# Two layers of a mixer and a feed-forward network in float32 on one core: low-rank products and key norm by tokens, and other banks and factor times where stages join

## The chip, the core and the metric

The kernel runs on one core of a Trainium2 chip. TensorE (PE) multiplies matrices into PSUM, VectorE (DVE), ScalarE (ACT) and GpSimd (POOL) work element by element, SyncE (SP) issues most transfers. Times are device microseconds of one execution. Each version runs several times; the median counts. One execution is also recorded by the hardware profiler: the profile and the trace are of that one.

## The reference, cut to what matters

256 tokens of width 1024 go through two layers. A layer adds to h a mixer of four branches (RWKV-7, dilated attention, mLSTM, HGRN-2, each gated and projected), then a gated feed-forward network of width 2816. All is float32.

```
for l in range(2):
    xn = rmsnorm(h, norm_mix_g[l]); z = xn @ w_in[l]
    merged = sum over 4 branches of sigmoid(gate_b + b_gate) * (y_b @ p_b)
    h = h + merged @ w_out[l]
    xn = rmsnorm(h, norm_ffn_g[l])
    u, gt = split(causal_dwconv(xn @ w_up[l])); h = h + (silu(gt) * u) @ w_down[l]
out = rmsnorm(h, final_norm_g)

# RWKV branch: what the change touches
logw = -softplus(-(w0 + tanh(wl) @ w2)) - 0.5      # wl, al: 32 wide; gl: 64 wide
a = sigmoid(a0 + al @ a2);  g = sigmoid(gl) @ g2
kk = k * k_k;  kk = kk * rsqrt(sum over a head's 64 columns of kk*kk + 1e-12)
```

## The kernel before, in words

**Weights.** All weights stream from HBM in 312 groups, most of 128 x 1024 float32 (raw, three buffers). For each product ACT rounds a group to the PE's one-pass type (hi, L301), DVE subtracts to get the rest (lo, L302), and each product is three matmuls: hi with the left high half, lo with it, hi with the left low half (mm3, L351 to L353). hi and lo have four buffers each. A request for group i issues transfers up to i + 6 and splits up to i + 4.

**Order.** The program text is in one sequence; a scheduler sets the order on each engine when the kernel is built, by priorities, so an edit in one stage can move rows on all engines. Work of the branches runs as background generators (rwkv, hgrn, attn, mlstm) that a step in the weight products advances. An engine runs its rows in that fixed order: a row whose inputs are late holds up all rows behind it on that engine.

**Norms by factor.** A norm is not applied to h ahead of a product. First products of a layer take u = (xh, xl), h times the norm's gain, and the result is multiplied by the row factor R when it is taken from PSUM. The factor: ACT squares h, sums into acc (L418); row_factor multiplies acc by ones on PE (psrm or psrf, L424), DVE scales (rcm, L426), POOL raises to -1/2 (L427); row_bcast spreads rcm over partitions with two float32 matmuls with an identity (psbm, L434) and ACT copies (Rm, L437). Later products take s = (sh, sl), blocks of h times gain and R (scaled_block, split_scaled, L440 to L454).

**Start of a layer (rw_cols, L605).** The RWKV columns are four groups of products, rw0 to rw3 (weight groups 0 to 6 in layer 0, 157 to 163 in layer 1), in three PSUM banks of the pool pmm that all stages share; zr takes them with R (L610). Between those evacuations stand the eight scaled blocks xsc. In layer 0 row_factor follows rw1 and R is made after the first half of rw2; in layer 1 row_factor follows rw0 and R stands within rw1. Then come the HGRN columns (hgq, hgf, and hgt by tokens), and after them gate products (gate). A second PSUM pool (PS["rw"], PS["mx"]) holds small tiles.

**RWKV's low-rank part (L669 to L734).** lort (the three low-rank matrices) and the activations are split by casts into lw and la, stacked so that hi and lo products sum in one matmul of 96 rows; psw and psa are two matmuls each, psg four. The key norm multiplies squares rsq (256 columns a token) by a block-diagonal matrix of ones on PE (pss), then ACT takes Ln and Exp with -0.5 (nk, L733 and L734, two table loads). Vt holds the values by tokens, copied by ACT from transposes (pv, L773, L781).

**Feed-forward.** 22 pairs of groups up0 to up21; the first five take u, R comes after up1's first half; POOL multiplies xsc by Rf and subtracts halves; then conv, silu, product af and its split ahi, alo (L1453 to L1459). In layer 1 the last product is by tokens, two row halves h by two column halves q (pso), and finish and emit add h, sum squares (ss), take the power and scale (L1492 to L1509).

Of the kernel before, what the change touches and what calls it, by code (L numbers as in the profile page):

```python
# [221 lines left out]
def trunk(tc, x, wst, prm, rows, lora, fing, cfd, cid, out, dbg=None, depth=DEPTH):  # L222
# [160 lines left out]
    def tok_group(name, cols, mid=None):  # L383

        pss = [pmm.tile([128, 512], F32, name=f"{name}{h}", tag="mm") for h in range(2)]
        for kh in range(4):
            hi, lo = w_next()
            for h in range(2):
                for k in range(2):
                    kk = kh * 2 + k  # L390
                    mm3(pss[h][:, :cols], X["s"][0][:, kk, h * 128:(h + 1) * 128], X["s"][1][:, kk, h * 128:(h + 1) * 128],
# [100 lines left out]
    for l in range(depth):  # L492
        with ExitStack() as lx:
# [12 lines left out]
            with ExitStack() as mxs:  # L506
# [48 lines left out]
                def project(b, kn, m2, quiet=False):  # L555
# [18 lines left out]
                    if m2 == 0:  # L574
                        mop = mp("mop", bufs=1)
                        pad(mop, "padm", 128)
                        X["m"] = (mop.tile([128, KB, T], F32R, name="mh"), mop.tile([128, KB, T], F32R, name="ml_"))
# [25 lines left out]
                R = None  # L603

                def rw_cols():  # L605
                    nonlocal R
# [5 lines left out]
                    def scale(ms):  # L612
                        for m in ms:
                            if m % 2 == 0:
                                tmp = gtp.tile([128, 2, T], F32, name="xsc", tag="gt")
                            scaled_block(m, P("gmix", m) if l else pr0[:, m:m + 1], R, tmp[:, m % 2, :])

                    u = X["u"]
                    ps0 = ct_group("rw0", outer=(l > 0), a=u)
                    rc = None  # L620
# [29 lines left out]
                def rwkv():  # L650
# [18 lines left out]
                    lw = rw.tile([128, 4, 256], F32R, name="lw", tag="bk")  # L669
                    hi_ = lambda d, s_: ac.copy(d, s_)  # L670
                    lo_ = lambda d, s_, h_: ve.tensor_tensor(d, s_, h_.bitcast(F32), op=OP.subtract)
                    for i, r in ((0, 0), (1, 32)):
                        src = lort[r:r + 32, :]
# [881 lines left out]
```

## Time and profile before

| what | value |
|---|---|
| median of 3 runs | 955.33 us (949.43 to 957.17) |
| the profiled execution | 955.37 us |
| its span | 953.5 us |
| granted PE clock in it | 0.993 of full speed |
| PE, DVE, ACT, POOL busy | 97%, 76%, 60%, 24% |
| instructions | 22170 |

The profile shows by engine how much of the span it was busy, who waited for whom, the chain of waits that ends last, and in a timeline each row with its start and length in us. In square brackets stands how long the engine stood idle ahead of a row and what it waited for last. A row may stand for several instructions (x4). A matmul's length contains its way through the array; starts of consecutive rows are closer together.

### The profile page before, as it was taken

The page shows a single profiled execution, that of the slowest core. Times are in us where ns is not written, and L with a number is a line of the kernel's source. Part 1 is how long each engine was busy: PE and PEld are TensorE (multiplying, and loading weights), DVE is VectorE, ACT ScalarE, POOL GpSimd, SP SyncE. Part 2 cuts the span into 40 slices and gives each one's busy share as a digit, 9 for nine tenths or more (in the row PEclk, how much of TensorE's full clock was granted, in tenths as well). Part 3 has the DMA queues.
Part 4 walks back from the last instruction along what each step waited for, and adds up shares of the span by engine and source line. Part 5 has one row for each costly group of instructions (what it writes and reads, how often), then busy time and mean ns, then how long its engine had stood idle before and what let it go on. Part 6 is the DMA issues. An engine that isn't in the chain of part 4 may idle for free.

```text
span 953.5 us, 22170 instructions
## 1 busy us (share of the span) xinstructions
PE 928.6 (97%) x9072; PEld 880.2 (92%) x9072; DVE 720.6 (76%) x1136; ACT 569.7 (60%) x968; POOL 226.3 (24%) x226
## 2 busy tenths in 40 slices
PE   8899999999999999999999999999999999999996
PEld 6888999999999999999998899999989999999885
DVE  6898566678688998876678975567768889988643
ACT  7784455665466676664478644555745667866533
POOL 2500141111317621110142004211103474211002
PEclk9999999999999999999999999999999999999998
DMA  7544444345475476556555434444536646656561
GB/s 276 177 135 132 126 149 142 134 154 166 144 216 183 146 221 199 187 174 197 189 172 181 147 98 125 154 155 122 188 123 189 201 138 215 230 189 200 182 193 66
DMA packets 48981, 160.12 MB, mean 168 GB/s; under 512 B 5872, under 2 KB 7408, under 8 KB 48752
## 3 DMA queue, kind: packets, MB, share of 16 engines
q1 hardware_dynamic: 46800, 155.03, 50.9%
q10 hardware_dynamic: 1728, 2.62, 0.9%
q8 instruction: 71, 1.16, 0.5%
q0 software_dynamic: 352, 1.06, 0.4%
q14 instruction: 30, 0.25, 0.1%
HBM read 156.06 MB, written 1.05 MB: 165 GB/s over the span
## 4 chain that ended last, share of the span: by engine, by line
PE 74%; DVE 10%; ACT 5%; POOL 4%; issue 4%; DMA 2%; POOLq 0%; SPq 0%; ACTq 0%; DVEq 0%
PE up L353 6%; PE up L351 6%; PE up L352 6%; PE gate L351 6%; PE gate L353 5%; PE gate L352 5%; PE dn L351 4%; PE dn L353 4%; PE dn L352 4%; DVE lo L302 4%; POOL sl L446 2%; POOL xsc L1432 2%; ACT hi L301 2%; DMA raw<-in_wst_dram 1%; PE at L351 1%
## 5 line engine op out<-in xcount | busy, mean ns | idle before, releaser
L302 DVE TENSOR_TENSOR lo<-raw,hi 128x1024 fp32r<-128x1024 f32 (+4 forms) x316 | 377.8, 1201 | 164.7 <-ACT hi L301 155.7
L301 ACT CAST hi<-raw 128x1024 fp32r<-128x1024 f32 (+4 forms) x316 | 307.4, 978 | 275.2 <-PE up L352 47.8
L353 PE MATMUL up<-sh,lo 128*128 128x256 f32 x544 | 152.2, 280 | 0.8 <-DVE lo L302 0.8
L351 PE MATMUL up<-sh,hi 128*128 128x256 f32 x544 | 152.0, 279 | 0.0
L352 PE MATMUL up<-sl,hi 128*128 128x256 f32 x544 | 151.9, 279 | 0.0
L351 PE MATMUL gate<-sh,hi 128*128 128x256 f32 x512 | 146.5, 286 | 0.0
L353 PE MATMUL gate<-sh,lo 128*128 128x256 f32 x512 | 143.0, 279 | 0.0
L352 PE MATMUL gate<-sl,hi 128*128 128x256 f32 x512 | 142.6, 279 | 0.0
L353 PEld LDWEIGHTS up<-sh,lo 128*128 128x128 f32 x544 | 103.4, 190 | 1.4 <-DVE lo L302 1.4
L352 PEld LDWEIGHTS up<-sl,hi 128*128 128x128 f32 x544 | 102.2, 188 | 0.0
L351 PEld LDWEIGHTS up<-sh,hi 128*128 128x128 f32 x544 | 102.2, 188 | 0.0
L351 PEld LDWEIGHTS gate<-sh,hi 128*128 128x128 f32 x512 | 96.5, 188 | 2.3 <-issue 0.2
L353 PEld LDWEIGHTS gate<-sh,lo 128*128 128x128 f32 x512 | 96.2, 188 | 0.6
L352 PEld LDWEIGHTS gate<-sl,hi 128*128 128x128 f32 x512 | 96.3, 188 | 0.4
L1457 POOL TENSOR_TENSOR af<-sf,cvf 128x256 f32<-128x256 f32 x44 | 45.9, 1043 | 157.8 <-ACT sf L1455 157.8
L1453 DVE SCALAR_TENSOR_TENSOR cvf<-up,pr,cvf 128x255 f32<-128x255 f32 (+1 forms) x136 | 65.1, 479 | 2.4
L572 POOL TENSOR_TENSOR merged<-merged,gt 128x512 f32<-128x512 f32 x16 | 26.6, 1666 | 114.3 <-DVE gt L570 114.3
L352 PE MATMUL dn<-alo,hi 128*128 128x256 f32 x176 | 49.5, 281 | 0.0
L353 PE MATMUL dn<-ahi,lo 128*128 128x256 f32 x176 | 49.5, 281 | 0.0
L351 PE MATMUL dn<-ahi,hi 128*128 128x256 f32 x176 | 49.4, 281 | 0.0
L352 PE MATMUL up<-xl,hi 128*128 128x256 f32 x160 | 44.8, 281 | 0.0
L353 PE MATMUL up<-xh,lo 128*128 128x256 f32 x160 | 44.6, 280 | 0.1
(468 smaller groups left out, 2370.0 us busy)
## 6 DMA issues: line engine op xcount, KB each, us to landing
raw<-in_wst_dram SPq DMA_DIRECT2D x254, 512.0 KB, 3.5
raw<-in_wst_dram SPq DMA_DIRECT2D x16, 448.0 KB, 3.2
raw<-in_wst_dram SPq DMA_DIRECT2D x26, 256.0 KB, 2.8
raw<-in_wst_dram SPq DMA_DIRECT2D x8, 392.0 KB, 3.2
zrot<-zrot ACTq DMA_DIRECT2D x24, 64.0 KB, 3.1
cft<-in_cf_dram SPq DMA_DIRECT2D x1, 1041.0 KB, 7.4
hT<-in_x_dram SPq DMA_DIRECT2D x4, 256.0 KB, 6.0
raw<-in_wst_dram SPq DMA_DIRECT2D x8, 128.0 KB, 2.6
```

Of the source, the lines that this page charges most:

```text
L301: ac.copy(hi[:, c], r[:, c])
L302: ve.tensor_tensor(lo[:, c], r[:, c], hi[:, c].bitcast(F32), op=OP.subtract)
L351: te.matmul(o, lh, rh, start=first, stop=False)
L352: te.matmul(o, lh, rl, start=False, stop=False)
L353: te.matmul(o, ll, rh, start=False, stop=last)
L446: gp.tensor_tensor(lo[:, m, :], tmp, h[:, m, :].bitcast(F32), op=OP.subtract)
L572: gp.tensor_tensor(mo, mo, g, op=OP.add)
L1432: gp.tensor_tensor(xsc[:, m, :], xsc[:, m, :], R, op=OP.mult)
L1453: ve.scalar_tensor_tensor(cv[:, n, d:], z[:, n, 0:T - d], P("fcw", 44 * i + cj), cv[:, n, d:], op0=OP.mult, op1=OP.add)
L1457: gp.tensor_tensor(a_, s, cv[:, 0, :], op=OP.mult)
```

## The change

In the RWKV branch psw, psa and psg become plain float32 matmuls of lort and the activations; lw, la and their casts and subtractions go. The key norm is taken by tokens: four float32 matmuls of 128 squares with two columns of ones (psn), DVE adds 1e-12, POOL raises to -1/2 (rn), and eight float32 matmuls with an identity spread it over partitions (pnk), from where DVE multiplies; Ln, Exp and their table loads go. In rw_cols rw2 and rw3 use banks of PS["rw"] in place of pmm; R follows the whole of rw1 in layer 1 and the middle of rw2 holds row_factor in layer 0. The scaled blocks move behind the evacuations into hg_cols. hgf and hgt take u in both layers, and the row factor is applied at evacuation (rc, and rch for the Tanh). In the feed-forward, up0 uses pmm, row_factor moves into the middle of up1 and R behind it. At the end the last 512 columns are two blocks of 256 (po2), each summed and added into ss as it ends; the other product with gr for the second token half moves from POOL to DVE. padm is 32 bytes.

The diff:

```diff
--- before.py
+++ after.py
@@ -363,7 +363,7 @@
...
-        pl = PS["mx"] if pool_tag == "mx" else pmm
+        pl = PS[pool_tag] if pool_tag else pmm
@@ -600,24 +601,23 @@
...
+                def scale(ms):
@@ -630,20 +630,19 @@
...
-                        ps1 = ct_group("rw1", a=u, mid=get_R)
+                        ps1 = ct_group("rw1", a=u)
+                        get_R()
...
-                        get_rc()
-                        ps2 = ct_group("rw2", a=u, mid=get_R)
+                        ps2 = ct_group("rw2", a=u, mid=get_rc, pool_tag="rw")
+                        get_R()
...
-                    scale(range(0, 4))
...
-                    scale(range(4, 8))
-                    evac(2, ps2 or ct_group("rw2", a=u))
+                    evac(2, ps2 or ct_group("rw2", a=u, pool_tag="rw"))
...
-                    ps = pmm.tile([128, 2, T], F32, name="rw3", tag="mm")
+                    ps = PS["rw"].tile([128, 2, T], F32, name="rw3", tag="rw")
@@ -666,38 +665,17 @@
...
-                        hi_(lw[0:32, i], src)
-                        hi_(lw[32:64, i], src)
-                        lo_(lw[64:96, i], src, lw[r:r + 32, i])
-                    hi_(lw[64:128, 2], lort[64:128, :])
-                    hi_(lw[0:64, 2], lort[64:128, :])
-                    lo_(lw[64:128, 3], lort[64:128, :], lw[64:128, 2])
...
-                        te.matmul(psw[:, n, :], lw[0:96, 0, n * 128:(n + 1) * 128], la[0:96, 0], start=True, stop=True)
-                        te.matmul(psa[:, n, :], lw[0:96, 1, n * 128:(n + 1) * 128], la[0:96, 1], start=True, stop=True)
+                        te.matmul(psw[:, n, :], lort[0:32, n * 128:(n + 1) * 128], lr[0:32, :], start=True, stop=True)
+                        te.matmul(psa[:, n, :], lort[32:64, n * 128:(n + 1) * 128], zm[32:64, 6, :], start=True, stop=True)
@@ -714,24 +692,26 @@
...
-                        te.matmul(psg[:, h, :], la[:, 2, h * 128:(h + 1) * 128], lw[:, 2], start=True, stop=False)
-                        te.matmul(psg[:, h, :], la[64:128, 2, h * 128:(h + 1) * 128], lw[64:128, 3], start=False, stop=True)
+                        te.matmul(psg[:, h, :], lr[64:128, h * 128:(h + 1) * 128], lort[64:128, :], start=True, stop=True)
...
-                    pss = PS["rw"].tile([128, 2, T], F32, name="pss", tag="rw")
-                    te.matmul(flat(pss), C("bd"), flat(sq), start=True, stop=True)
+                    psn = PS["rw"].tile([128, 2, 2, 2], F32, name="psn", tag="rw")
+                    for h in range(2):
+                        for n in range(2):
+                            te.matmul(psn[:, h, n, :], sq[:, n, h * 128:(h + 1) * 128], C("ind"), start=True, stop=True)
...
+                    ve.tensor_scalar(rn[:, 0, :], psn.rearrange("p h n q -> p (h n q)"), 1e-12, None, op0=OP.add)
+                    gp.tensor_tensor(rn[:, 1, :], rn[:, 0, :], nhalf, op=OP.pow)
...
-                    ac.activation(nk, pss, AF.Ln, bias=eps12)
-                    ac.activation(nk, nk, AF.Exp, scale=-0.5)
@@ -750,8 +730,16 @@
...
+                    pnk = PS["rw"].tile([128, 2, T], F32, name="pnk", tag="rw")
+                    for n in range(2):
+                        for h in range(2):
+                            for q in range(2):
+                                i = h * 4 + n * 2 + q
+                                te.matmul(pnk[q * 64:q * 64 + 64, n, h * 128:(h + 1) * 128], rn[:, 1, i:i + 1].to_broadcast([128, 64]),
+                                          ident, start=True, stop=True)
...
-                    ve.tensor_tensor(kk, kkr, nk, op=OP.mult)
+                    ve.tensor_tensor(kk, kkr, pnk, op=OP.mult)
@@ -952,20 +940,19 @@
...
-                        ps = ct_group("hg" + nm, **({"a": X["u"]} if direct else {}))[0][1]
+                        ps = ct_group("hg" + nm, a=X["u"])[0][1]
...
-                            ve.tensor_tensor(z, ps, bc2(R, 2), op=OP.mult)
...
+                        ve.tensor_tensor(z, ps, bc2(R, 2), op=OP.mult)
...
-                    pss = tok_group("hgt", 512)
+                        scale(range(i * 4, i * 4 + 4))
+                    pss = tok_group("hgt", 512, a=X["u"])
+                    rch = zp.tile([128, 2], F32, name="rch")
+                    ve.tensor_scalar(rch, rc[:, 0:2], 0.5, None, op0=OP.mult)
...
-                        ac.activation(V[:, h, :], pss[h][:, 0:256], AF.Copy)
-                        ac.activation(tg[:, h, :], pss[h][:, 256:512], AF.Tanh, scale=0.5)
+                        ac.activation(V[:, h, :], pss[h][:, 0:256], AF.Copy, scale=rc[:, h:h + 1])
+                        ac.activation(tg[:, h, :], pss[h][:, 256:512], AF.Tanh, scale=rch[:, h:h + 1])
@@ -1414,14 +1401,10 @@
...
-                        ps0 = ct_group("up0", outer=True, quiet=True, pool_tag="mx", a=u)
-                        rc = row_factor(f"f{l}")
-                        def get_R():
...
-                            R = row_bcast(f"f{l}", rc)
-                        ps1 = ct_group("up1", quiet=True, pool_tag="mx", a=u, mid=get_R)
+                        ps0 = ct_group("up0", outer=True, quiet=True, a=u)
+                        rcf = []
+                        ps1 = ct_group("up1", quiet=True, pool_tag="mx", a=u, mid=lambda: rcf.append(row_factor(f"f{l}")))
+                        R = row_bcast(f"f{l}", rcf[0])
@@ -1477,35 +1460,42 @@
...
-                    pso = [[PS["mx"].tile([128, 512], F32, name=f"dn{h}{q}", tag="mx") for q in range(2)] for h in range(2)]
+                    pso = [[PS["mx"].tile([128, 512], F32, name=f"dn{h}{q}", tag="mx") for q in range(2 - h)] for h in range(2)]
+                    po2 = {part: pmm.tile([128, 256], F32, name=f"dn11{part}", tag="mm") for part in (0, 256)}
...
+                                mm3(po2[part], ahi[:, k, t], alo[:, k, t], hi[:, c], lo[:, c], k == 0, k == NJ - 1)
...
-                        ve.tensor_tensor(o_, pso[h][q], htt[:, h, c], op=OP.add)
...
+                        ve.tensor_tensor(o_[:, b], po2[b0] if h and q else pso[h][q], htt[:, h, c], op=OP.add)
...
-                        ac.activation(sq, o_, AF.Square, accum_out=ss[:, q:q + 1])
+                        ac.activation(sq[:, b], o_[:, b], AF.Square, accum_out=ss[:, i:i + 1])
+                        ve.tensor_scalar(ss[:, 4 + i:5 + i], ss[:, i:i + 1], 1.0 / D, ss[:, 3 + i:4 + i] if i else 1e-6, op0=OP.mult, op1=OP.add)
...
-                            gp.tensor_tensor(o_, o_, gr[:, c], op=OP.mult)
...
-                        ve.tensor_tensor(ss[:, 2:3], ss[:, 0:1], ss[:, 1:2], op=OP.add)
-                        ve.tensor_scalar(ss[:, 2:3], ss[:, 2:3], 1.0 / D, 1e-6, op0=OP.mult, op1=OP.add)
...
+                            (ve if h else gp).tensor_tensor(o_[:, b], o_[:, b], gr[:, c], op=OP.mult)
...
+                        gp.tensor_tensor(r, ss[:, 4 + i:5 + i], nhalf[:, 0:1], op=OP.pow)
```

On PE, at the start of layer 0, before: psrm (L424) stands 27 rows above psbm; the rows here are those around psbm, with hi4 and lo4 as weight group 4 (rw2).

```order
L353 MATMUL rw2_351<-xh_112,lo4_233 128x256
L351 MATMUL rw2_351<-xh_112,hi5_265 128x256
L352 MATMUL rw2_351<-xl_113,hi5_265 128x256
L434 MATMUL psbm0_383<-ident_t_70,rcm0_348 128x128 x2
L353 MATMUL rw2_351<-xh_112,lo5_266 128x256
```

Now, in the same place: psrm follows the last row of rw1 and psbm follows it by two rows of rw2. The 24 rows of rw2 that stood between psrm and psbm follow psbm.

```order
L353 MATMUL rw1_260<-xh_112,lo3_202 128x256
L425 MATMUL psrm0_377<-ones_77,acc_84 128x1 x2
L351 MATMUL rw2_345<-xh_112,hi4_232 128x256
L352 MATMUL rw2_345<-xl_113,hi4_232 128x256
L435 MATMUL psbm0_413<-ident_t_70,rcm0_380 128x128 x2
L353 MATMUL rw2_345<-xh_112,lo4_233 128x256
```

DVE at the start of layer 0, before (rcm is the row factor by tokens, zr the RWKV columns, xsc the scaled blocks, lo4 to lo8 the low halves of weight groups):

```order
L302 TENSOR_TENSOR lo4_233<-raw4_193,hi4_232 128x1024
L426 TENSOR_SCALAR rcm0_348<-psrm0_345 128x2
L302 TENSOR_TENSOR lo5_266<-raw5_195,hi5_265 128x1024
L302 TENSOR_TENSOR lo6_318<-raw6_230,hi6_317 128x1024
L302 TENSOR_TENSOR lo7_356<-raw7_263,hi7_355 128x1024
L302 TENSOR_TENSOR lo8_391<-raw8_315,hi8_390 128x1024
L610 TENSOR_TENSOR zr_185<-rw0_187,Rm0_386 128x2x256
L454 SCALAR_TENSOR_TENSOR xsc_419<-hT_73,pr0_71,Rm0_386 128x256
L454 SCALAR_TENSOR_TENSOR xsc_430<-hT_73,pr0_71,Rm0_386 128x256
L610 TENSOR_TENSOR zr_185<-rw1_260,Rm0_386 128x2x256
L454 SCALAR_TENSOR_TENSOR xsc_439<-hT_73,pr0_71,Rm0_386 128x256
L454 SCALAR_TENSOR_TENSOR xsc_447<-hT_73,pr0_71,Rm0_386 128x256
```

And now: both zr and the four scaled blocks stand ahead of lo6, and rch behind lo4. Before, lo4 to lo8 stood ahead of all of them.

```order
L427 TENSOR_SCALAR rcm0_380<-psrm0_377 128x2
L302 TENSOR_TENSOR lo4_233<-raw4_193,hi4_232 128x1024
L950 TENSOR_SCALAR rch_819<-rcm0_380 128x2
L302 TENSOR_TENSOR lo5_266<-raw5_195,hi5_265 128x1024
L617 TENSOR_TENSOR zr_185<-rw0_187,Rm0_416 128x2x256
L617 TENSOR_TENSOR zr_185<-rw1_260,Rm0_416 128x2x256
L455 SCALAR_TENSOR_TENSOR xsc_567<-hT_73,pr0_71,Rm0_416 128x256
L455 SCALAR_TENSOR_TENSOR xsc_578<-hT_73,pr0_71,Rm0_416 128x256
L455 SCALAR_TENSOR_TENSOR xsc_680<-hT_73,pr0_71,Rm0_416 128x256
L455 SCALAR_TENSOR_TENSOR xsc_688<-hT_73,pr0_71,Rm0_416 128x256
L302 TENSOR_TENSOR lo6_318<-raw6_230,hi6_317 128x1024
L302 TENSOR_TENSOR lo7_350<-raw7_263,hi7_349 128x1024
```

ACT at the start of layer 1, before (hi161 to hi164 are weights, Rm1 the row factor spread over partitions, xsc the scaled blocks):

```order
L670 CAST lw_6849<-lort_6498 64x256 x2
L301 CAST hi161_6533<-raw161_6440 128x1024
L301 CAST hi162_6594<-raw162_6525 128x1024
L301 CAST hi163_6629<-raw163_6531 128x1024
L437 COPY Rm1_6625<-psbm1_6622 128x256
L451 ACTIVATE xsc_6670<-hT_73,pr_6483 128x256
```

And now: Rm1 stands behind hi164, one cast later than before. In the feed-forward of both layers Rf likewise moved behind one more cast.

```order
L301 CAST hi162_6587<-raw162_6518 128x1024
L301 CAST hi163_6617<-raw163_6524 128x1024
L301 CAST hi164_6656<-raw164_6585 128x1024
L438 COPY Rm1_6648<-psbm1_6645 128x256
L452 ACTIVATE xsc_6871<-hT_73,pr_6476 128x256
L452 ACTIVATE xsc_6973<-hT_73,pr_6476 128x256
```

## Rows read from the trace of the kernel before

**Rows 1.** The chain that ended last, by engine, from the page.

```profile
PE 74%; DVE 10%; ACT 5%; POOL 4%; issue 4%; DMA 2%; POOLq 0%; SPq 0%; ACTq 0%; DVEq 0%
```

**Rows 2.** Waits of PE: line, releaser: us in total, times, longest.

```profile
PE rw L351 <- DVE zr L610: 4.0, 2, 2.7
...
PE pv L773 <- ACT Vt L781: 1.8, 2, 1.1
...
PE psrf L424 <- DVE acc L418: 1.4, 2, 1.2
...
PE up L353 <- DVE lo L302: 0.8, 3, 0.4
```

**Rows 3.** Timeline of PE, start of layer 0: start, length, what [idle before].

```profile
22.21 0.61 PE L424 MATMUL psrm<-ones,acc 128*128 128x1 f32 x4 [0.58 <-DVE acc L418]
...
23.49 0.39 PE L353 MATMUL rw<-xh,lo 128*128 128x256 f32 x1 [0.33 <-DVE lo L302]
...
26.34 0.61 PE L434 MATMUL psbm<-ident_t,rcm 128*128 128x128 f32 x4
26.70 0.37 PE L353 MATMUL rw<-xh,lo 128*128 128x256 f32 x1
...
32.20 0.40 PE L351 MATMUL rw<-xh,hi 128*128 128x256 f32 x1 [2.65 <-DVE zr L610]
```

**Rows 4.** Stretches: length, busy time of each engine, granted clock, DMA share, GB/s.

```profile
33.00:36.50 3.50, 3.50 (x19) 3.50 (x19) 3.50 (x6) 3.17 (x9) 3.50 (x5) 0.53 0.40 140
```

**Rows 5.** Timeline of ACT, start of layer 0.

```profile
29.24 1.04 ACT L301 CAST hi<-raw 128x1024 fp32r<-128x1024 f32 x1 [0.76 <-DMA raw<-in_wst_dram]
30.19 0.37 ACT L437 COPY Rm<-psbm 128x256 f32<-128x256 f32 x1
```

**Rows 6.** Timeline of DVE, start of layer 0.

```profile
31.46 0.69 DVE L610 TENSOR_TENSOR zr<-rw,Rm 128x512 f32<-128x512 f32 x1
32.06 1.93 DVE L454 SCALAR_TENSOR_TENSOR xsc<-hT,pr,Rm 128x256 f32<-128x256 f32 x2
```

**Rows 7.** Timeline of PE around psw and around psg and pss.

```profile
47.17 0.36 PE L699 MATMUL psw<-la,lw 96*128 96x256 f32 x1 [0.48 <-DVE la L671]
...
53.61 0.39 PE L351 MATMUL hgt<-hi,sh 128*128 128x512 f32 x1
53.84 0.28 PE L717 MATMUL psg<-lw,la 128*128 128x256 f32 x1
...
54.98 1.13 PE L726 MATMUL pss<-rsq,cft 128*128 128x512 f32 x2
...
56.18 0.40 PE L353 MATMUL hgt<-hi,sl 128*128 128x512 f32 x1
```

**Rows 8.** Timeline of PE: two small float32 products elsewhere.

```profile
89.59 0.95 PE L807 MATMUL psq<-cft,prod 128*128 128x2 f32 x8
...
228.40 1.57 PE L1309 MATMUL pS<-cv 64*128 64x256 f32 x12
```

**Rows 9.** Groups of ACT by line: count, busy us, mean ns.

```profile
L670 ACT CAST lw<-lort 32x256 fp32r<-32x256 f32 (+1 forms) x12 | 4.8, 403 | 1.8 <-DMA lort<-in_lora_dram 1.6
...
L733 ACT ACT_TABLE_LOAD x2 | 2.6, 1283 | 0.0
```

**Rows 10.** Timeline of POOL: the power of the row factor.

```profile
23.59 1.62 POOL L427 TENSOR_TENSOR rcm<-rcm,nhalf 128x2 f32<-128x2 f32 x1 [2.42 <-DVE rcm L426]
```

**Rows 11.** Stretches behind the starts of layers 0 and 1, columns as above.

```profile
50.00:75.00 25.00, 24.86 (x219) 21.23 (x217) 22.89 (x44) 19.94 (x34) 0.00 (x0) 1.00 0.52 159
525.00:550.00 25.00, 23.93 (x257) 21.71 (x256) 23.14 (x46) 16.63 (x31) 0.86 (x2) 1.00 0.43 136
```

**Rows 12.** Timeline after the last matmul, of DVE and POOL.

```profile
945.52 0.69 DVE L1492 TENSOR_TENSOR o__12474<-dn,htt 128x512 f32<-128x512 f32 x1 [0.64 <-PE dn L353]
...
947.06 0.64 DVE L1500 TENSOR_TENSOR ss<-ss 128x1 f32<-128x1 f32 x1 [0.85 <-ACT osq L1494]
...
947.97 0.55 POOL L1502 TENSOR_TENSOR ss<-ss,nhalf 128x1 f32<-128x1 f32 x1 [0.29 <-DVE ss L1501]
```

More of the change, by code (lines that the diff above doesn't have):

```diff
@@ L381, in ct_group, with tok_group @@
         return [(slice(0, 2), ps)]
-    def tok_group(name, cols, mid=None):
+    def tok_group(name, cols, mid=None, a=None):
+        ah, al = a or X["s"]
         pss = [pmm.tile([128, 512], F32, name=f"{name}{h}", tag="mm") for h in range(2)]
@@ L390, in tok_group @@
                     kk = kh * 2 + k
-                    mm3(pss[h][:, :cols], X["s"][0][:, kk, h * 128:(h + 1) * 128], X["s"][1][:, kk, h * 128:(h + 1) * 128],
+                    mm3(pss[h][:, :cols], ah[:, kk, h * 128:(h + 1) * 128], al[:, kk, h * 128:(h + 1) * 128],
                         hi[:, k * cols:(k + 1) * cols], lo[:, k * cols:(k + 1) * cols], kk == 0, kk == 7)
@@ L575, in project @@
                         mop = mp("mop", bufs=1)
-                        pad(mop, "padm", 128)
+                        pad(mop, "padm", 32)
                         X["m"] = (mop.tile([128, KB, T], F32R, name="mh"), mop.tile([128, KB, T], F32R, name="ml_"))
@@ L601, in trunk @@
                 gp.memset(zr[:, :, 0:1], 0.0)
-                R = None
+                R = rc = None
+                def scale(ms):
+                    for m in ms:
+                        if m % 2 == 0:
+                            tmp = gtp.tile([128, 2, T], F32, name="xsc", tag="gt")
+                        scaled_block(m, P("gmix", m) if l else pr0[:, m:m + 1], R, tmp[:, m % 2, :])
                 def rw_cols():
-                    nonlocal R
+                    nonlocal R, rc
                     def evac(g, ps):
@@ L1486, in down, with finish @@
                         t = slice(h * 128, h * 128 + 128)
+                        if h and q:
+                            for part in parts:
+                                c = slice(512 + part, 768 + part)
+                                mm3(po2[part], ahi[:, k, t], alo[:, k, t], hi[:, c], lo[:, c], k == 0, k == NJ - 1)
+                            return
                         mm3(pso[h][q], ahi[:, k, t], alo[:, k, t], hi[:, c], lo[:, c], k == 0, k == NJ - 1)
-                    def finish(h, q, ss):
-                        c = slice(q * 512, q * 512 + 512)
-                        o_ = op_.tile([128, 512], F32, name="o_", tag=f"o{h}{q}")
-                        ve.tensor_tensor(o_, pso[h][q], htt[:, h, c], op=OP.add)
+                    def finish(h, q, ss, o_, b0=0, b1=512, i=0):
+                        b, c = slice(b0, b1), slice(q * 512 + b0, q * 512 + b1)
+                        ve.tensor_tensor(o_[:, b], po2[b0] if h and q else pso[h][q], htt[:, h, c], op=OP.add)
@@ L1504, in emit @@
+                        return i
+                    def emit(h, o2, ss, i):
+                        r = ss[:, 8:9]
+                        gp.tensor_tensor(r, ss[:, 4 + i:5 + i], nhalf[:, 0:1], op=OP.pow)
+                        ac.activation(o2[0], o2[0], AF.Copy, scale=r)
                         nc.scalar.dma_start(out[0, h * 128:(h + 1) * 128, 0:512], o2[0])
                         if h == 0:
-                            ac.activation(o2[1], o2[1], AF.Copy, scale=ss[:, 3:4])
+                            ac.activation(o2[1], o2[1], AF.Copy, scale=r)
@@ L1517, in trunk @@
                     for h in range(2):
-                        ss = op_.tile([128, 4], F32, name="ss", tag=f"ss{h}")
-                        o2 = []
+                        ss = op_.tile([128, 10], F32, name="ss", tag=f"ss{h}")
+                        o2 = [op_.tile([128, 512], F32, name="o_", tag=f"o{h}{q}") for q in range(2)]
                         for q in range(2):
-                            for k in range(NJ - 4, NJ):
-                                down(k, h, q)
-                            o2.append(finish(h, q, ss))
-                        emit(h, o2, ss)
+                            for part in (0, 256) if h and q else (0,):
+                                for k in range(NJ - 4, NJ):
+                                    down(k, h, q, (part,) if h and q else ())
+                                if h and q:
+                                    i = finish(h, q, ss, o2[q], part, part + 256, 1 + part // 256)
+                                else:
+                                    i = finish(h, q, ss, o2[q], i=q)
+                        emit(h, o2, ss, i)
             tap(f"h2_{l}", flat(hT))
```

38 lines of the change are left out of this document (4 added, 34 removed).

## The prediction

> **What bounds the kernel now.** I read the chain of waits first: TensorE (PE) holds 74% of it, VectorE (DVE) 10%, ScalarE (ACT) 5% [rows 1]. So time is won where PE stands still, or where it is given less to do; relief for ACT counts only where PE waits for what ACT is late with. The second view is PE's waits [rows 2]. Those that the change touches are small: 4.0 us on zr in two waits, 1.8 on Vt in two, 1.4 on the sum of squares ahead of psrf in two, and 0.8 on the low half of a weight in three. The other entries lie in stretches in which PE's order does not change.
>
> The third view is the timeline of the start of layer 0. PE waits 0.58 us for the sum of squares, 0.33 for a low half, and 2.65 for zr [rows 3]; right behind the last it runs 3.5 us at a granted clock of 0.53, about the lower of its two levels (1.2 of 2.4 GHz) [rows 4]. It has 19 matmul records there; at the upper level, where a 512-column matmul takes 0.23 us (53.61 to 53.84, [rows 7]) and one of 256 columns so 0.117, 3.5 us hold 30. The 11 that are missing are 1.3 us, and I put 1.5, since records that lap over an end of the stretch are counted among the 19. Why zr is late stands in ACT's queue: the copy of the row factor Rm sits behind the cast of weight 8, which waited 0.76 us for its transfer, and runs at 30.19 [rows 5], though its matmuls were done at 26.70 [rows 3]. DVE then multiplies zr at 31.46, and scaled blocks of 0.96 us each stand between that and the next zr [rows 6].
>
> **The change part by part.** Everything is set against the profiled execution: 955.37 us, a span of 953.5 and 1.9 around it. The median of the three runs is 955.33, so no shift is needed.
>
> *Product work on PE, each layer.* Removed: psw and psa, four one-pass matmuls of 0.117 us behind the 0.36 of a first one that starts late (47.17): about 0.55; psg from 53.84 to 54.98, 1.14; pss from 54.98 to the second hgt matmul at 56.18, less the 0.23 that one hgt matmul takes (53.61 to 53.84), 0.97 [rows 7]. Together 2.66. Added: six plain float32 products of 256 columns. The nearest row is pS, which is float32 too: 12 records, eight of them (four products) of 256 columns and four (two products) of 128, in 1.57 us [rows 8]. By columns that is 1.57/5 = 0.31 for 256; I take 0.30, so 1.8. psn has the shape of psq, whose eight records (four matmuls with two columns) took 0.95 [rows 8]. pnk is eight products of 128 columns; psbm, two of these, ran from 26.34 to 26.70 [rows 3], so 8 x 0.18 = 1.44, half of it if the two 64-row halves run beside each other. Sum 4.2, net +1.5 a layer, **+3.1** in both. Bounds: +1.6 with paired pnk; +5.1 if each float32 product is 0.47 us instead, as much as four one-pass matmuls of 0.117, one for each pairing of high and low halves. All of this lies on the path: PE is busy 24.86 of 25 us from 50 to 75 [rows 11], and the waits elsewhere are counted below.
>
> The Trainium skill, "FP8 and Floating Point Precision", section "TensorE Precision Notes", states that true float32 takes four passes through the array. By it the sum is 2.0 us higher. The trace speaks for less: pS shows two records a product and 0.31 us.
>
> *What ACT and DVE lose.* A layer loses six casts of lw and five of la at some 0.40 us and two table loads at 1.28 [rows 9], 7 us off ACT, and the Ln and Exp themselves; six subtractions go off DVE. On the path this is worth only the wait on la (0.48, [rows 7]) and what Vt is late for (1.8 in all, the longer 1.07, so 0.73 in layer 0; [rows 2] gives 1.1): ACT has slack elsewhere. psw now waits for the Tanh of zr instead, so I give none of the 0.48 back; of Vt I give half back.
>
> *Start of layer 0.* Before, 0.58 + 0.33 + 2.65 + 1.5 + 0.48 + 0.73 = 6.3 us is lost. Now psbm stands two matmuls behind psrm instead of 26, so the way psrm, DVE 0.15, power on GpSimd (POOL), psbm lies open: 0.6 for psrm + 0.15 + 1.62 for the power [rows 10], less 0.7 of PE work, 1.7 to 1.8 of waiting. On the other side Rm has three casts fewer ahead of it and is copied about 5 us earlier. Then DVE does both zr (1.4) and four scaled blocks (3.9) ahead of the low half of weight 6 (1.2). With psbm at 24.7 and Rm at 25.6 that half is done at about 32.1; PE, with 50 matmuls of 0.118 us behind psbm, gets there at about 31.0. I take 1.3 for that wait, with the hand-overs. With 0.5 for psw and 0.35 for Vt 4.0 are lost, **-2.2** after rounding. Bounds: -5 (both new waits covered), +2 (the clock falls behind both).
>
> The power took 1.62 us beside DVE's subtraction of weight 4, and 0.55 at the end of the kernel where DVE stands still [rows 10, 12]. With 0.55 the first wait would be 0.7, and the sum 1.1 lower. I take 1.62: DVE's order still puts that subtraction right behind the 0.15 step. The Trainium skill, "SBUF — State Buffer", section "Who interferes with whom", gives a rule for this: a DVE instruction with two SBUF inputs and a GpSimd read exclude each other, and whoever issued first keeps the port. The two rows agree with it.
>
> *Start of layer 1.* Before 1.35 (zr: 4.0 less 2.65) + 1.07 (Vt) [rows 2, 3]. Now weight 164 is cast ahead of Rm, a cast of 1.04 ([rows 5]) that may have to wait for its transfer as weight 8's did in layer 0; so Rm comes 1 to 2 us later than before, but 24 + 48 matmuls of rw3 and hgq no longer need a bank that zr must free. I take 0.8 for what is left of waits, about half of Vt included: **-1.2** (2.4 - 0.8 would be -1.6; I hold back 0.4 for the later Rm). Bounds -2.4 and +1.
>
> *Feed-forward.* Of 2.2 us (psrf 1.4, three low halves 0.8, [rows 2]) the first goes: psrf moves into the middle of the second group. But Rf is copied one cast later, about 1.35 us (a cast of 1.04 [rows 5] and the gap), and POOL's and DVE's chain behind it shifts; and low halves are late there already ([rows 2]), so I count one of 0.5 in each layer: **-1.1** after rounding. Bounds -2.2, +0.5 (each Rf's 1.35 in full).
>
> *End.* After the last matmul: an addition of 0.69, ACT's square behind it, an addition of two sums 0.64 with 0.85 idle ahead of it, then the power 0.55 [rows 12]. Halving the last block takes about 0.27 off the addition and, an estimate from that 0.85, 0.2 off the square; folding the sum takes 0.64 out, 1.1 together. PE pays 132 matmuls of 256 columns for 66 of 512, at 0.117 and 0.23 about +0.3. **-0.7**; bounds 0 and -1.1.
>
> Sum: 3.1 - 2.2 - 1.2 - 1.1 - 0.7 = -2.1, that is **953.3 us**. Layout of the SBUF pad, scaled hgt factors at evacuation and the like I cost at nothing: they change operands of instructions that were there, on engines with slack.
>
> **The rivals.** *A, the new order at the starts gives nothing (slower).* Place: DVE's queue at the start of each layer. If the low half of weight 6 (layer 0) ends 3.6 us or more after PE gets there, the half-clock stretch of 1.5 comes with it, the 6.3 us come back in full, and in layer 1 the late Rm returns 2.4; the feed-forward waits come back as well. Left is +3.1 - 0.7 = +2.4: 957.8; with 0.47 for a float32 product 959.8. For: DVE is at 22.89 and 23.14 of 25 us in 50 to 75 and 525 to 550 [rows 11], and the change moves its scaled blocks ahead of two low halves. Against: these are 5.3 us of DVE work that PE has 46 matmuls to cover.
>
> *B, everything goes.* The power runs free, pnk pairs, weight 6 is in time, no low half is late: 1.6 - 5 - 2.4 - 2.2 - 1.1 = -9.1: 946.3. Against: each would need a queue with slack at the same moment.
>
> *C, the clock.* Two waits of 1.8 and 1.3 within 8 us might bring the half clock as 2.65 did: +1.5, 954.8. For: [rows 4]. Against: the wait of 1.35 in layer 1 (4.0 less 2.65, [rows 2, 3]) had no such stretch behind it. The Trainium skill, "TensorE: Matmul & The Clock Gate", section "HAM oscillation — how this bites in real kernels", says that waits between bursts bring the slower level again and again; the trace agrees for the 2.65 wait only.
>
> *D, four passes:* +2.0, 955.3, worked out above from 0.117 us a pass. Against: pS [rows 8].
>
> **How the numbers follow.** Forecast 0.50 (own range 950 to 956.5), A 0.22, C 0.10, D 0.08, B 0.07, others 0.03. No single measurement of this kernel tells a change within 1% (9.5 us) from none; its three runs lie from 949.43 to 957.17. The range runs from 947.5, between the forecast's low end and B, to 960.0, just past A's high end. Only B's far side lies under 945.8 and only a loss beyond A's over 964.9: faster 0.05, same 0.91, slower 0.04.
>
> **What would show it.** psw/psa, psg, psn and pnk on PE's timeline: starts to starts of 0.30, and 1.4 for pnk. psbm's wait behind psrm near 1.7 with POOL's power beside a subtraction; Rm before 27 us; a wait of PE on the low half of weight 6 near 1.3; no wait on zr. No psrf wait; one late low half in each feed-forward. From the last matmul to the last issue about 1.1 us less. I am wrong if the zr wait is replaced by one as long on another row, if the clock is halved again, or if time moves in the middle of the layers, where no PE row has changed place.

## The result, and the profile after

| | kernel before | changed kernel |
|---|---|---|
| median | 954.72 us (949.43 to 960.25, 18 runs) | 947.38 us (945.86 to 950.19, 18 runs) |
| ratio | 1 | 0.993, 95% interval 0.9914 to 0.9947 |
| profiled execution, span | 955.37, 953.5 | 946.59, 944.4 |
| granted PE clock in it | 0.993 | 0.997 |

The change makes the kernel 0.7% faster by the ratio, some 6.7 us; the forecast was 2.1. A second series of both kernels gave 0.9953 (0.9917 to 0.9989), 4.5 us. The page of the changed kernel, its engines and its chain, answers to [rows 1]:

```profile
PE 921.4 (98%) x9190; PEld 874.8 (93%) x9190; DVE 714.4 (76%) x1132; ACT 554.4 (59%) x939; POOL 226.9 (24%) x227
...
PE 81%; DVE 7%; POOL 4%; DMA 4%; issue 2%; ACT 2%; SPq 0%; ACTq 0%; DVEq 0%; POOLq 0%
```

PE holds more of the chain, 81%, and DVE less, 7%. Its waits answer to [rows 2]:

```profile
PE up L353 <- DVE lo L302: 2.6, 2, 1.7
PE pv L761 <- ACT Vt L769: 1.8, 2, 1.1
PE psbm L435 <- POOL rcm L428: 1.6, 1, 1.6
...
PE rw L353 <- DVE lo L302: 0.9, 1, 0.9
PE psg L695 <- ACT w4a L684: 0.7, 1, 0.7
```

The zr wait (4.0) and the psrf wait (1.4) are gone. In their place stand 1.6 on psbm, 0.9 on the low half of weight 6, 0.7 on psg, and low halves in the feed-forward went from 0.8 to 2.6. Vt is as late as before. Now the timeline of PE in the columns of layer 0, which answers to [rows 3, 7]:

```profile
22.83 0.71 PE L435 MATMUL psbm<-ident_t,rcm 128*128 128x128 f32 x4 [1.62 <-POOL rcm L428]
...
30.11 0.38 PE L353 MATMUL rw<-xh,lo 128*128 128x256 f32 x1 [0.88 <-DVE lo L302]
...
38.92 0.48 PE L677 MATMUL psw<-lr,lort 32*128 32x256 f32 x1
38.93 0.48 PE L678 MATMUL psa<-zr,lort 32*128 32x256 f32 x1
...
39.98 0.39 PE L353 MATMUL hgf<-xh,lo 128*128 128x256 f32 x1
...
44.19 1.13 PE L695 MATMUL psg<-lort,lr 64*128 64x256 f32 x4 [0.74 <-ACT w4a L684]
45.25 0.39 PE L351 MATMUL hgf<-xh,hi 128*128 128x256 f32 x1
...
46.74 0.95 PE L706 MATMUL psn<-cft,rsq 128*128 128x2 f32 x8
...
54.82 1.09 PE L739 MATMUL pnk<-ident_t,rn 128*64 128x128 f32 x16
55.84 0.34 PE L761 MATMUL pv<-ident_t,vT 128*128 128x128 f32 x1
```

psw and psa start in pairs 10 ns apart, on other rows of the array, and run beside each other: four products take 1.06 us (38.92 to 39.98). psg has two products, one behind the other, and takes 1.06 too (its next row starts at 45.25). psn takes 0.81 by starts and pnk 1.02 (54.82 to 55.84). Sum 3.95 against the 2.66 that went: **+1.3 a layer**.

POOL's power, ACT's copy and DVE's queue behind it answer to [rows 5, 6, 10]:

```profile
21.14 1.64 POOL L428 TENSOR_TENSOR rcm<-rcm,nhalf 128x2 f32<-128x2 f32 x1 [1.86 <-DVE rcm L427]
```

```profile
23.57 0.37 ACT L438 COPY Rm<-psbm 128x256 f32<-128x256 f32 x1 [2.11 <-PE psbm L435]
```

```profile
20.90 0.16 DVE L427 TENSOR_SCALAR rcm<-psrm 128x2 f32<-128x2 f32 x1 [0.70 <-PE psrm L425]
20.98 1.23 DVE L302 TENSOR_TENSOR lo<-raw,hi 128x1024 fp32r<-128x1024 f32 x1
...
24.03 1.28 DVE L617 TENSOR_TENSOR zr<-rw,Rm 128x512 f32<-128x512 f32 x2
25.23 3.14 DVE L455 SCALAR_TENSOR_TENSOR xsc<-hT,pr,Rm 128x256 f32<-128x256 f32 x4
28.29 1.76 DVE L302 TENSOR_TENSOR lo<-raw,hi 128x1024 fp32r<-128x1024 f32 x1
```

The power takes 1.64 us beside the subtraction of weight 4, which DVE issued 0.16 us before it; Rm is there at 23.6 instead of 30.2; both zr and four blocks stand ahead of the low half of weight 6. The order is as forecast, and the copy is 2 us ahead of the 25.6 that was reckoned with. The end answers to [rows 12]:

```profile
935.51 1.80 DVE L1487 TENSOR_TENSOR o__12486<-o__12486,gr 128x512 f32<-128x512 f32 x1
...
936.03 0.28 PE L353 MATMUL dn<-hi,alo 128*128 128x256 f32 x1
...
937.36 0.41 DVE L1482 TENSOR_TENSOR o__12487<-dn,htt 128x256 f32<-128x256 f32 x1
...
938.70 0.55 POOL L1492 TENSOR_TENSOR ss<-ss,nhalf 128x1 f32<-128x1 f32 x1 [0.95 <-DVE ss L1485]
...
939.28 0.75 DVE L1498 SCALAR_TENSOR_TENSOR o__12487<-o__12487,ss,gr 128x512 f32<-128x512 f32 x1 [0.67 <-POOL ss L1492]
```

The last matmul starts at 936.03 and the last addition only at 937.36: DVE is at a product with gr of 1.80 us, which the change took from POOL. Before, that distance was 0.43 us. From there it is shorter, but from the last matmul to the end of the span there are 8.4 us before and 8.3 after.

**How the difference of the two profiles divides.** Waits of layer 0's start: 4.8 before, 4.3 after; of layer 1's start 2.4 and 0.7; of the feed-forwards 2.2 and 2.6; ahead of the w_out products 0.4 and 1.3. With +2.6 for the products that is +1.7 us. So by these waits and this work alone the changed kernel would be slower. Against that stand 1.5 us for the half-clock stretch behind zr, 1.0 ahead of the first product, and 5.1 by a pace of the matmuls that I had not known of (the last section).

A further term lies where the prediction had no PE row changing place: in the small float32 products pl (RWKV) and pdl (HGRN), for the most part between gate and psq. Here are rows of layer 0, before and then after:

```profile
77.01 1.16 PE L792 MATMUL pl<-ar,bk 64*128 64x128 f32 x8
78.10 0.30 PE L1074 MATMUL pdl<-qsb,kt 64*64 64x32 f32 x4
```

```profile
75.03 1.16 PE L780 MATMUL pl<-ar,bk 64*128 64x128 f32 x16
76.12 0.67 PE L1061 MATMUL pdl<-qsb,kt 64*64 64x32 f32 x32
```

Eight rows of pl alone take 1.09 us (77.01 to 78.10); sixteen that stand together start in pairs, one on the upper and one on the lower 64 rows of the array, and take 1.09 us too (75.03 to 76.12). Before, pl stands in four groups and pdl in 13 in each layer; after, in three and eight. By starts the two take 10.6 us a layer before and 8.1 after, with as many matmuls, in both traces of either kernel apart from stretches at the lower clock. pdg, another product of the HGRN branch, takes 0.3 a layer more without its waits, so the term is -4.4 in both layers. With it the terms come to about 1 us more than the 9.1 between the two spans, so some are counted twice or too high. Two traces therefore don't tell what the change is worth. Below, each series gives the clock of every execution, and I use its **deficit**, (1 - granted clock) x span, averaged over the runs. It also counts 1.4 to 3.0 us at the end of the span. Runs over 1.5% longer than the fastest of their kernel are left out of the means.

### The profile page after: what moved, and what is told of

It is laid out like the page before. It is cut to its first block, busy times and chain, and to the rows that moved or that the text cites. A ratio compares the mean times of both kernels' runs of the same rounds, so it can differ in the third digit from the quotient of the medians.

```text
span 944.4 us, 22367 instructions
## 1 busy us (share of the span) xinstructions
PE 921.4 (98%) x9190; PEld 874.8 (93%) x9190; DVE 714.4 (76%) x1132; ACT 554.4 (59%) x939; POOL 226.9 (24%) x227
## 3 DMA queue, kind: packets, MB, share of 16 engines
q0 software_dynamic: 352, 1.06, 0.4%
## 4 chain that ended last, share of the span: by engine, by line
PE 81%; DVE 7%; POOL 4%; DMA 4%; issue 2%; ACT 2%; SPq 0%; ACTq 0%; DVEq 0%; POOLq 0%
PE up L353 7%; PE up L351 7%; PE up L352 6%; PE gate L351 6%; PE gate L353 6%; PE gate L352 6%; PE dn L351 4%; PE dn L353 4%; PE dn L352 4%; DMA raw<-in_wst_dram 3%; DVE lo L302 3%; POOL xsc L1415 2%; POOL sl L447 2%; PE at L351 1%; PE pp L351 1%
```

## The experiments

"Only" kernels are the kernel before with one part of the change, "no" kernels the changed one with a part undone. Ratios are to the kernel before in the same series; dividing the mean times gives values up to 0.1% away.

| kernel | ratio (95% interval) | deficit, mean | mean time, kernel and before |
|---|---|---|---|
| e1 before again | 0.9995 (0.9954 to 1.0036) | 10.2 | 956.7, 956.5 |
| e2 change again | 0.9953 (0.9917 to 0.9989) | 5.6 | 952.0, 956.5 |
| e3 feed-forward only | 0.9970 (0.9932 to 1.0007) | 8.3 | 953.4, 956.5 |
| e4 no feed-forward | 0.9951 (0.9921 to 0.9980) | 5.7 | 952.1, 956.5 |
| e5 starts only | 1.0038 (1.0006 to 1.0070) | 9.4 | 960.0, 955.8 |
| e6 low-rank only | 0.9936 (0.9901 to 0.9971) | 5.6 | 951.5, 955.8 |
| e7 end only | 0.9984 (0.9957 to 1.0011) | 9.4 | 955.2, 955.8 |
| e8 no low-rank | 1.0034 (1.0002 to 1.0066) | 9.3 | 959.2, 955.8 |
| e9 products only | 0.9945 (0.9916 to 0.9974) | 8.0 | 949.4, 954.4 |
| e10 key norm only | 1.0013 (0.9985 to 1.0041) | 6.9 | 956.5, 954.4 |
| e11 low-rank with lw | 0.9990 (0.9960 to 1.0020) | 5.5 | 953.7, 954.4 |
| e12 low-rank and end | 0.9984 (0.9958 to 1.0011) | 5.9 | 952.1, 954.4 |

The kernel before has deficits of 9.6, 8.7 and 8.0 in the three series (e1 to e4, e5 to e8, e9 to e12).

**e1 and e2: the same two kernels again.** No edit.

> The kernel before, unchanged, for a second trace. The first two traces differ in more than waits: between 303.7 and 488.5 us of the kernel before, one-pass matmuls of 256 columns start 118 ns apart, while in the changed kernel they start 113 ns apart there; that alone is some 6.4 us of the 9.1 between the two spans. Theory P (the pace is drawn anew in each execution, whatever the kernel): the slow-paced stretch lies elsewhere in this trace or is missing, and the span follows it: 949 to 951 us with none in the feed-forward of layer 0, 955 to 957 with one. Theory Q (the place of the row factor in the feed-forward sets the pace): the stretch from psbf of layer 0 to the start of layer 1 is at 118 again. Ratio 1.000 either way.

> The changed kernel, unchanged, for a second trace. Theory P: the stretches at 118 ns lie elsewhere than in its first trace (there 210 to 232, 480 to 523, 671 to 693), and a long one may stand in either feed-forward; spans between 944 and 948. Theory Q: both feed-forwards are at 113 again. Waits the same by both: 1.6 us on psbm, 0.9 on the low half of weight 6, 1.0 and 1.7 on low halves in the two feed-forwards. Ratio 0.993.

Measured: the long stretch at 118 ns is missing in the second trace of before. Stretches of 25 us in its layer 0 feed-forward, in the first and the second trace of the same kernel (length, busy time of PE with its count of records, weight loads, DVE, ACT, POOL, granted clock, DMA share, GB/s):

```profile
340.00:365.00 25.00, 25.00 (x215) 25.00 (x214) 23.32 (x37) 18.95 (x31) 5.23 (x6) 1.00 0.76 227
365.00:390.00 25.00, 25.00 (x215) 25.00 (x214) 19.81 (x32) 16.08 (x27) 4.71 (x5) 1.00 0.59 184
```

```profile
340.00:365.00 25.00, 25.00 (x223) 25.00 (x222) 23.93 (x39) 19.77 (x33) 5.13 (x5) 1.00 0.78 228
365.00:390.00 25.00, 25.00 (x223) 25.00 (x222) 20.73 (x33) 16.95 (x30) 4.90 (x5) 1.00 0.65 198
```

PE is busy throughout, at a granted clock of 1.00, and gets through 215 records or 223. So the same kernel has the long stretch in one execution and not in the next, and theory Q is out. That the pace has nothing to do with the kernel, the other half of theory P, is not shown: the three kernels with the whole low-rank part and the old starts (e6, e11, e12) have 214 or 215 records in these windows, each in its one trace, all other kernels 223; and in the changed kernel shorter slow stretches come back (210 to 232 and 671 to 693 us in its first trace, 214 to 235 and 674 to 696 in its second). The span of e1, 955.2, is not the 949 to 951 that P gave for a trace without the long stretch, since the lower clock costs more instead:

```profile
34.00:38.00 4.00, 4.00 (x21) 4.00 (x20) 4.00 (x6) 2.99 (x9) 4.00 (x5) 0.50 0.13 53
...
546.00:550.00 4.00, 4.00 (x22) 3.64 (x22) 1.92 (x2) 1.16 (x3) 0.00 (x0) 0.50 0.32 103
```

Behind the zr wait, here 3.1 us, the clock is at 0.50 for 6.8 us, and from 542 to 554, among the small products of layer 1, for 10.2. e2's span of 948.9 is a little past the 944 to 948 of P, and its waits are those expected. The changed kernel's mean time is 4.5 us less than that of before, of which the deficit makes 4.0.

**e3 and e4: the feed-forward part.**

```
-  ps0 = ct_group("up0", outer=True, quiet=True, pool_tag="mx", a=u); rc = row_factor(f"f{l}")
-  ps1 = ct_group("up1", quiet=True, pool_tag="mx", a=u, mid=get_R)
+  ps0 = ct_group("up0", outer=True, quiet=True, a=u)
+  ps1 = ct_group("up1", ..., mid=lambda: rcf.append(row_factor(f"f{l}"))); R = row_bcast(f"f{l}", rcf[0])
```

e3 has these lines, e4 has all others.

> The kernel before with only the feed-forward part of the change (up0 in pmm, psrf in the middle of up1, R behind it). By waits alone (theory P): psrf's 1.4 us go, low halves come late for 1 to 1.7 in each layer, so within 1 us of before, ratio 0.999 to 1.002. Theory Q: the pace of the layer 0 feed-forward goes to 113, ratio 0.993 to 0.995.

> The changed kernel with the feed-forward part undone (up0 and up1 in one pool, psrf between them, R in the middle of up1). By waits alone (theory P): psrf's waits of 1.2 and 0.3 come back and the late low halves of 1.0 and 1.7 go, so 0.5 to 1.5 us faster than the changed kernel, ratio to the kernel before 0.991 to 0.993. Theory Q: the layer 0 feed-forward is at 118 again, 6 us slower than the changed kernel, ratio 0.998 to 1.000.

Measured: 0.997 alone, and with or without it in the changed kernel 0.9953 and 0.9951. The row of e4's waits "psrf, 1.9 us in two" and e2's "up on lo, 2.7 in two" are the trade: the psrf wait turns into late low halves. e3 and e4 lie between the ranges of the two theories, so they don't decide between them (the trace of e1 does). The part is worth nothing that these series can show.

**e5 to e8: starts, low-rank part, end, and the change without the low-rank part.** e5 has the diff's lines in rw_cols and hg_cols, e6 those from lw to pnk, e7 those of pso to emit.

> The kernel before with only the starts of the layers changed (rw2 and rw3 in other banks, R where the change has it, scaled blocks behind, hgf and hgt from u). So far: over their executions (1 - granted clock) x span is 9.6 us on average for the kernel before and 5.6 for the changed one, and the times without it are within 0.6 us of each other; the gain is time at the lower clock level that no longer occurs. Theory S (the zr wait of layer 0, 2.65 to 3.1 us, is what brings the lower level): this kernel gets most of it, clock loss 5.5 to 7, ratio 0.994 to 0.997. Theory L (the RWKV branch does: in two traces of before the lower level holds from 542 to 554, among its small products): clock loss stays at 9 or more, ratio 0.998 to 1.001.

> The kernel before with only the float32 low-rank products and the key norm by tokens. Theory S: clock loss stays at 8.5 to 10, the added product work of 3.1 us stays, ratio 1.001 to 1.004. Theory L: clock loss falls to 5 to 7, the stretch 542 to 554 is at the upper level, ratio 0.995 to 0.999.

> The kernel before with only the end changed (last 512 columns in two blocks). Both theories: clock loss as before, 0.7 us faster, ratio 0.999; from the last matmul to the last transfer's issue 1.1 us less than the 4.2 before.

> The changed kernel with the low-rank products and key norm as before. Theory S: clock loss 5 to 6 as in the changed kernel and 3.1 us of product work fewer, ratio to the kernel before 0.990 to 0.993. Theory L: clock loss back at 8 to 10, ratio 0.997 to 1.000.

Measured: theory L by its direction. The low-rank part alone brings all of it (0.9936), the rest without it makes the kernel slower (1.0034), and so do the starts alone (1.0038), by more than either theory had said. e5's waits of PE show why:

```profile
PE psw L698 <- DVE la L670: 4.5, 1, 4.5
...
PE psw L698 <- ACT mixt L657: 3.3, 1, 3.3
```

With the starts changed, PE gets to psw before la is there: it waits 4.5 us for la and, in layer 1, 3.3 for mixt, a step of ACT on the way to la, where the kernel before waited 0.48 and not at all. In e8 the same two waits are 4.1 and 2.7. The zr wait is gone and these stand in its place. And the copy that I had put down to the starts did not come: in e5, Rm is still copied at

```profile
29.74 1.05 ACT L301 CAST hi<-raw 128x1024 fp32r<-128x1024 f32 x1 [1.73 <-DMA raw<-in_wst_dram]
30.69 0.37 ACT L438 COPY Rm<-psbm 128x256 f32<-128x256 f32 x1
```

behind the casts of weights 7 and 8, as in [rows 5]. In e6, which leaves rw_cols as it was, psbm stands two matmuls behind psrm, as in the changed kernel:

```profile
20.61 0.61 PE L424 MATMUL psrm<-ones,acc 128*128 128x1 f32 x4
21.08 0.36 PE L351 MATMUL rw<-xh,hi 128*128 128x256 f32 x1
21.28 0.28 PE L352 MATMUL rw<-xl,hi 128*128 128x256 f32 x1
23.18 0.71 PE L434 MATMUL psbm<-ident_t,rcm 128*128 128x128 f32 x4 [1.62 <-POOL rcm L427]
```

Rm is copied at 23.93, and DVE does two zr and four blocks ahead of the low half of weight 6 there too. The order at the start of layer 0 that the prediction priced as the work of the starts is made by the low-rank part. e7, the end alone, gains nothing that its series can show: the 8.4 us from the last matmul to the end of its span are those of before, where 1.1 less had been expected.

**e9 to e12: what of the low-rank part, and a combination.** e9 keeps pss and nk. e10 keeps lw and la and has psn and pnk. e11 is e6 with these lines back, in another buffer, with nothing reading lw:

```
+  for i, r in ((0, 0), (1, 32)):
+      hi_(lw[0:32, i], src); hi_(lw[32:64, i], src); lo_(lw[64:96, i], src, lw[r:r + 32, i])
+  hi_(lw[64:128, 2], lort[64:128, :]); hi_(lw[0:64, 2], lort[64:128, :]); lo_(...)
```

e12 is e6 and e7 together.

> The kernel before with only psw, psa and psg in float32 (no lw, no la); the key norm as before with Ln and Exp. The low-rank part as a whole gave 0.9936 with a clock loss of 5.5 us against 8.9. Theory U (the casts of lw stand in ACT's and DVE's queues at the start of layer 0, ahead of the squares; without them the row factor is earlier, psbm moves up, the long zr wait goes, and with it the lower clock behind it): this kernel gets most of the gain, 0.993 to 0.996, clock loss 5 to 6.5. Theory M (the gain is made in the middle, by ACT's lighter key norm ahead of the small products of layers 0 and 1): 0.998 to 1.001, clock loss 8 to 10.

> The kernel before with only the key norm by tokens; psw, psa and psg from split halves as before. Theory U: start of layer 0 as before with the zr wait of 2.6 to 3.2, clock loss 8 to 10, product work of psn and pnk added, ratio 1.000 to 1.003. Theory M: 0.994 to 0.997, clock loss 5 to 7.

> The kernel with only the low-rank part changed, but the casts and subtractions of lw are put back and nothing reads their result. They take 2.4 us of ACT and 1.3 of DVE in each layer; the order at the start of layer 0 is again that of before (psbm 26 matmuls behind psrm, Rm behind three casts more). Theory U: zr wait and clock loss of before come back, 8 to 10 us, ratio 0.998 to 1.002. Theory M: gain kept, 0.994 to 0.996, clock loss 5 to 6.5.

> The kernel before with the low-rank part and the end of the change, without the changed starts and feed-forward. If the parts add up (0.9936 and 0.9984), ratio 0.991 to 0.993, faster than the whole change (0.993 and 0.995 in its two series), since the changed starts alone cost 0.4%. If the starts only cost where la is late, as with split products, the whole change has lost nothing by them and this kernel is at 0.993 to 0.996 like it.

Measured: the products bring the gain (0.9945), the key norm none (1.0013), and with lw back the ratio is 0.9990. That is the direction of theory U, though the intervals of e9 and e11 still touch (up to 0.9974 and from 0.9960). What U names is in the timelines of ACT, of before, of e11 and of e9:

```profile
16.84 2.51 ACT L670 CAST lw<-lort 32x256 fp32r<-32x256 f32 x6
```

```profile
16.34 0.50 ACT L415 ACTIVATE sq<-hT,dummy 128x256 f32<-128x256 f32 x1
16.75 2.51 ACT L670 CAST lw<-lort 32x256 fp32r<-32x256 f32 x6
...
20.64 0.51 ACT L415 ACTIVATE sq<-hT,dummy 128x256 f32<-128x256 f32 x1 [0.45 <-POOL acc L416]
```

```profile
15.99 0.90 ACT L415 ACTIVATE sq<-hT,dummy 128x256 f32<-128x256 f32 x2
...
18.82 0.51 ACT L415 ACTIVATE sq<-hT,dummy 128x256 f32<-128x256 f32 x1 [0.18 <-POOL acc L416]
```

In e11 the six casts of lw, 2.51 us, stand between the squares at 16.75, so the last square is at 20.64 instead of 18.82. PE's rows follow, e11 first:

```profile
22.13 0.61 PE L424 MATMUL psrm<-ones,acc 128*128 128x1 f32 x4 [0.60 <-DVE acc L418]
...
31.95 0.39 PE L351 MATMUL rw<-xh,hi 128*128 128x256 f32 x1 [2.49 <-DVE zr L610]
```

```profile
22.87 0.71 PE L434 MATMUL psbm<-ident_t,rcm 128*128 128x128 f32 x4 [1.62 <-POOL rcm L427]
```

The 2.49 us for zr are there with lw and gone without it. The waits of PE of 0.2 us and more, without those on pp and warmup that all kernels have, add up to 11.3 us before, 5.8 in e6, 7.0 in e9 and 9.9 in e11. So in the traces the return of lw costs some 4 us of waits.

But U is not all. First, pl and pdl: they take 16.2 us in both layers together in e9, in e11 and in the changed kernel, 21.2 before and 20.3 in e10. So the products bring this gain too, about as large as that of the waits, and the return of lw does not undo it. No run here takes the two apart, nor did one ask what regroups these rows.

Second, the deficit goes another way: 8.0 in e9, which has the gain, and 5.5 in e11, which hasn't. It goes with the key norm by tokens: the kernels that have it (e2, e4, e6, e10, e11, e12 and the changed one) lie between 5.0 and 6.9, those without between 8.0 and 10.2. By mean times less deficits, e10 is 3.1 us dearer than before, of which psn and pnk less pss make 1.7 (2 x (0.81 + 1.02 - 0.97)): what the key norm gives back in clock it takes in work.

Third, e12, which should have been e6 and a little, is at 0.9984, no better than e11 and without lw. Its trace has the start of e6, waits of 6.4 us against 5.8 and about the same slow pace (13.8 and 14.2 us); nothing in it says why. So the parts do not add up within what these series resolve, about 0.3%, and no kernel here beats the whole change beyond doubt.

## Why the prediction came out as it did

The measured median of 947.4 us lies 0.1 below the low edge of the stated range, 947.5; the ratio of 0.993, put on 955.33, gives 948.6, inside it. The direction is right. The sum of -2.1 is a third of the 6.7 that the ratio gives; its parts erred both ways, and a large part of the gain came from places that it put at nothing.

- **Product work, +3.1.** Right: +2.6 by rows. The single price was wrong in both directions: a float32 product of 256 columns alone takes 0.53 us (psg), above the 0.47 of rival D; two on different rows of the array share that time (psw with psa, 0.265 each). pS, the row that I took, is made of such pairs. The four passes that the Trainium skill states ("FP8 and Floating Point Precision", section "TensorE Precision Notes") agree better with psg than my 0.30 does.
- **"On the path this is worth only the wait on la ... and what Vt is late for."** This step failed. I counted the casts of lw in layer 0 as slack and did not ask where they stand: at 16.84 us in ACT's queue, ahead of the last squares of the first norm. Without them psrm starts at 20.61 in e6, 1.6 us earlier than in [rows 3], and the scheduler puts psbm behind it. The changed order that I showed was real; what made it was the other part of the diff.
- **"... if time moves in the middle of the layers, where no PE row has changed place."** This failed too: pl and pdl are regrouped there and take 2.5 us a layer less, some 4.4 in all with pdg, a term that the sum has at nothing. The prediction named time moving there as a sign of being wrong.
- **Start of layer 0, -2.2.** The rows came as forecast: psbm 1.62 (1.7 to 1.8 said), low half of weight 6 0.88 (1.3), no zr. The 0.55 us of the power alone and its 1.64 here fit the rule of "SBUF — State Buffer", section "Who interferes with whom", in the Trainium skill once more: the 1.64 are beside DVE's subtraction, issued first. But as a part it is a loss: e5 is at 1.0038, since the wait turns up on psw. Rival A, a slower kernel, had such a wait in another place: it is what the starts do when la is still made.
- **Start of layer 1, -1.2.** -1.7 by rows, with the same partner: in e5 psw waits 3.3 us there.
- **Feed-forward, -1.1.** Failed: +0.4 by rows, nothing by e3 and e4. Rf one cast later costs 0.93 and 1.69 us of low halves, not 0.5 each.
- **End, -0.7.** Failed in the trace: nothing gained, since I left out the 1.80 us of a step that moves to DVE, though the diff shows it. e7's interval reaches from 4 us faster to 1 slower.
- **The clock.** I counted one half-clock stretch of 1.5 us as lost before and let it come back in rival C. Mean deficits of 8.0 to 10.2 us before and 5.0 and 5.6 in the changed kernel's two series make this 4.0 of the 4.5 us between the mean times of the second. It can't be read from one trace: before's first one has a stretch of 3.4 us at 9.0 us, while the first weights were loading, and one of 3.4 behind zr; its second has none at 9.0 but 20.5 us at the lower clock later, 6.8 of them behind zr. Which steps bring them is only partly shown: of six traces with the zr wait of layer 0, five have one behind it (before, e1, e3, e7, e10; not e11); of six with psbm's wait in its place, three (e4, e6, e9; not the changed kernel's two, nor e12); and e5 and e8 have one at psw's wait of 4.5 and 4.1. The Trainium skill's rule on waits between bursts ("TensorE: Matmul & The Clock Gate", section "HAM oscillation — how this bites in real kernels") agrees with the ten traces that have one, though the waits of the kernel it tells of are longer, about 3 to 5 us; that the same wait of 1.62 us has such a stretch behind it in one execution and none in another stands in the traces alone.

Open: why the key norm by tokens lowers the deficit, what regroups pl and pdl, what decides the pace, and how the parts interact below 0.3%.

## What to carry to other kernels

Ask of every instruction that a change removes where it stands in its queue, not where its result is used: casts of a small weight, hoisted to the start, held up the first norm. A wait that is removed goes to the next late input; price that input by its own chain before counting the gain. Small products on different rows of the array gain from standing beside each other, so compare PE's whole order, also where nothing was edited. And where a median moves by less than the kernel's own runs differ, one trace a side does not say why: compare the clock and the pace of several executions first.

## What was not expected of the hardware

**Two paces at one clock.** One-pass matmuls of 256 columns start 113 or 118 ns apart, in stretches of up to 188 us (301 to 489 in e6), at a granted clock of 1.00 in both. The long stretch of before begins behind the two small products psbf (303.2 us) and ends at psrm of layer 1 (487.9); in the next execution it is missing. Over the profiled executions, starts 115 to 128 ns apart cost between 4.8 us (change) and 14.2 us (e6) over 113.4 ns each, about the mean at the faster pace; the two traces of before have 9.9 and 5.3. What decides between the two is not known.

**The lower clock comes and goes between executions of one kernel.** Behind the first 20 us and ahead of the end, the time at 0.50 went from none (the change's first trace) to 23.9 us (e3, in stretches of 6.8, 3.4, 3.4 and 10.2).

**Float32 products on different rows run beside each other**, above: 1.06 us for four of 32 rows, 1.06 for two of 64 rows that stand alone, and 1.09 for sixteen rows of pl in pairs as for eight alone.
